# HGRN2 by running decay products and a state per 128 tokens, its levels spread between the other projections of the mixers

## The chip, the cores and the metric

One core of a Trainium2 chip runs the whole program. The metric is the device time of one execution in microseconds (us); lower is better. The engines are PE (TensorE, matrix products; PEld is its weight load), DVE (VectorE), ACT (ScalarE), POOL (GpSimd) and SP (SyncE, which here only issues DMAs). Each works through its own queue in order and waits for the others on semaphores.

## What is computed

A decoder of two layers over 512 tokens of width 1024, in fp32. Each layer is a gated MLP half step, four token mixers that share one input projection, a second half step, and a per-layer embedding:

```python
for l in range(DEPTH):
    h = h + 0.5 * swiglu(rmsnorm(h, ffn1_norm[l]), ...)
    z = rmsnorm(h, mix_norm[l]) @ w_in[l]
    (c_q, c_kv, k_pe, z_u, z_v, hq, hf, hi, hg, rq, rk, rv, rg) = jnp.split(z, ...)
    y_a = mla_mixer(c_q, c_kv, k_pe, ...)
    y_b = spatial_gating_mixer(z_u, z_v, ...)
    y_c = hgrn2_mixer(hq, hf, hi, hg, lb_all[l], hg_norm[l])
    y_d = retention_mixer(rq, rk, rv, rg, ...)
    h = h + jnp.concatenate([y_a, y_b, y_c, y_d], axis=-1) @ w_out[l]
    h = h + 0.5 * swiglu(rmsnorm(h, ffn2_norm[l]), ...)
    h = h + (p[l] @ ple_w_proj[l]) * jax.nn.sigmoid(rmsnorm(h, ple_norm[l]) @ ple_w_gate[l])
```

HGRN2, the mixer that the change rewrites, has 4 heads with keys of 128 and values of 64. It is a gated linear recurrence whose decay differs for each key channel and token:

```python
forget = lb + (1.0 - lb) * sigmoid(f);  log_f = log(forget);  k = 1.0 - forget
b = cumsum(log_f)                                   # over the tokens
scores[t, s] = sum_k q[t, k] * exp(b[t, k] - b[s, k]) * k[s, k]      # s <= t
o = scores @ v;   o = o * rsqrt(mean(o * o) + EPS) * norm_g;   y = o * silu(g)
```

(The reference cuts this into chunks of 64 tokens with a state between them; the sum is the same.)

## The kernel before

Activations lie feature-major: a tile is 128 features by 512 tokens, the hidden state is 8 such tiles `h`. Every projection is fp32 in three passes of the fp32r type: weights and inputs are each split into a high and a low part, and `mm3` issues high x high, high x low, low x high (the lines 142 to 144). A 128-column chunk of a projection is 8 x 3 = 24 matmuls of 512 columns into one PSUM bank. Weights come in tiles of 128 x 1024 by SP's queue (two raw buffers), are rounded to `wh` by ACT (L132) and get their rest `wl` from DVE (L133), three buffers each. The PSUM pool "d" (4 banks) takes the dense products (tiles z, n, uq, uk, uv, y), the pool "m" (4 banks) all small ones. What is said of dense work below means those `mm3` matmuls.

A scheduler sets the order of each engine's queue by the order of the program text and by priority; what stands under `urgent()` goes ahead, and `after(i, j)` fixes i behind j on its engine.

`mixers(l, ...)` runs once a layer. Chunks of the transposed input projection (`winT`, tile z) are 0 to 7 for HGRN2's f and q, 8 to 11 for MLA's latents, 12 to 15 for retention's q and k, 16 to 19 for the gates; `natural(j)` makes 512 token-major columns (tile n, 96 matmuls), j = 0 for the values of HGRN2 and retention, j = 1 for the spatial gating. In program order: `hgrn_gates(0)` (heads 0 and 1: tiles q, k, and c, the log of the forget gate), the latents, the values, `hgrn_scores` and `values_out` of the first pair of heads, `ret_rot` (retention's rotated q and k, copied into head order by 16 DMAs of POOL), MLA's projections and attention, `hgrn_gates(1)`, retention, HGRN2's second pair of heads, the gates and group norm of retention, `natural(1)` and the spatial gating, the gates and group norm of HGRN2, and the output projection. The z chunks of `hgrn_gates(1)`, 96 matmuls, are what PE has to do between attention's steps, and the z chunks of later steps and `natural(1)` are what lies between the second pair's levels.

`hgrn_scores` works by nine levels of halving. At level lev, tokens stand in blocks of w = 2^lev, and the second of two neighbours takes scores against the first. The tile `lev` holds both sides: q times exp of the log decay since the block's start, k times exp of what is left to the block's end. A level needs two ACT Exps, two DVE products (L500, L504), one DVE subtraction (L502) and one POOL addition onto c (L508), then its small matmuls: up to level 4, 32 products of 32 x 32 (`near`, tile nr, merged into `sc` by a predicated copy, L510), then 16, 8, 4 and 4 larger ones (tile lv), copied by ACT into the score tile `hst`. `values_out` sums values over the scores: per pair of heads 8 products of the diagonal 128-token blocks (L349) and 6 of all later tokens (L355), columns 128 to 384.

Of the kernel before, what the change touches and what calls it, by code (L numbers as in the profile page):

```python
# [19 lines left out]
P = 128  # L20
# [21 lines left out]
LN_MIN = 2.0**-60  # L42

# gain columns of vecs
# [10 lines left out]
# columns of cst  # L55
# [6 lines left out]
def trunk(ctx, tc, xT, pT, pos, wgu, wdn, winT, winN, wout, wpg, wpp, wmla,  # L62
# [24 lines left out]
    def stile(name="st"):  # L87
        return tp.tile([P, 10, P], F32, tag="st", bufs=5, name=nm(name))
# [75 lines left out]
    def split(src, g=None, name="x"):  # L164
        """parts of src * g"""
# [9 lines left out]
    def rsqrt(src, n):  # L175
        """(src + EPS) ** -0.5 of a few columns: a first guess from the exponent, then Newton steps"""
# [15 lines left out]
    def row_rsqrt(acc, n, last=None, v=None):  # L192
        """rsqrt(mean + eps) on all partitions, from the summed squares"""
# [9 lines left out]
    def ln_rsqrt(q, n, r, last=None, vt=None):  # L203
        """(q / n + EPS) ** -0.5 of full rows, by Ln and Exp and a Newton step"""
# [10 lines left out]
    def columns(r, tag):  # L215
        """rows on all partitions to columns, token by token"""
# [7 lines left out]
    class Norm:  # L224
        """operands and scale of RMSNorm(h) @ W, filled chunk by chunk"""
# [72 lines left out]
    tabs = {}  # L298

    def tables():  # L300
# [5 lines left out]
        def sine(dst, inv, phase, turn):  # L306
            """sin(pos * inv + phase), the argument reduced to [-pi, pi]"""
# [33 lines left out]
    def values_out(st, diag, v, hh):  # L341
        """[2 heads x 64, tok]: sum over s of v[s] st[s, t], two heads side by side in the array"""
# [16 lines left out]
    def group_norm(os, vx, gates, gcol):  # L359
        """parts of RMS norm per head * gain * gate, both chunks of a mixer; os lacks the queries' scale vx ** -0.5"""  # L360
# [13 lines left out]
        res = []  # L374
        dve.tensor_tensor(y, y, gates, op=ALU.mult)
        for c in range(2):
            dve.scalar_tensor_tensor(y[:, c], y[:, c], vec[:, gcol + c:gcol + c + 1], rr[:, c], op0=ALU.mult, op1=ALU.mult)
            res.append(split(y[:, c], name="yT"))
        return res

    def mixers(l, norm, done):
# [4 lines left out]
        def tchunk(j, wait=None):  # L386
            w = weights(winT[l, j])
            o = dense("z")
            for k in range(KD):
                i = mm3(o, wpart(w, k * P), xpart(x[k]), k == 0, k == KD - 1)  # L390
                if wait is not None and k == 0:
                    after(i, wait)
            return o

        def scaled(dst, j, wait=None):
            o = tchunk(j, wait)
# [3 lines left out]
        def natural(j, evac, wait=None):  # L400
            os = [dense("n") for _ in range(NB)]
            for b in range(4):
                w = weights(winN[l, 4 * j + b])
                for i in range(NB):
                    for e in range(2):
                        k = 2 * b + e
                        m = mm3(os[i], xpart(x[k], i * P, P), wpart(w, e * T, T), k == 0, k == KD - 1)
                        if wait is not None and k == 0:
                            after(m, wait)
# [8 lines left out]
        # lower bounds of the forget gates  # L418
        lbv = vec[:, C_LB:]
        if l:  # L420
# [14 lines left out]
            omlb = sp.tile([P, 4], F32, tag="omlb", bufs=1, name="omlb")  # L435
            dve.tensor_scalar(omlb, lb, -1.0, 1.0, op0=ALU.mult, op1=ALU.add)

        def hgrn_gates(b, wait=None):
            """q, k and log forget of two heads"""
            q, kk, c = unit(name="q"), unit(name="k"), unit(name="c")  # L440
            for e in range(2):
                hh = 2 * b + e
                f, n0 = kk[:, e], c[:, e]
                scaled(f, 4 * b + e, wait)
                act.activation(n0, f, AF.Relu, scale=-1.0)
                i = act.activation(f, f, AF.Relu)
                ea, eb, ls = t2(name="ea"), t2(name="eb"), t2(name="ls")
# [4 lines left out]
                after(act.activation(ea, n0, AF.Exp, scale=-1.0), i)  # L452
                after(act.activation(eb, f, AF.Exp, scale=-1.0), i)
                dve.tensor_tensor(ls, ea, eb, op=ALU.add)
                act.activation(ls, ls, AF.Ln)
                if l:
                    dve.scalar_tensor_tensor(n0, eb, lb[:, hh:hh + 1], ea, op0=ALU.mult, op1=ALU.add)
                    dve.tensor_scalar(n0, n0, LN_MIN, None, op0=ALU.max)
                    act.activation(n0, n0, AF.Ln)
                    dve.tensor_tensor(n0, n0, ls, op=ALU.subtract)  # L460
                else:
                    dve.scalar_tensor_tensor(n0, n0, -1.0, ls, op0=ALU.mult, op1=ALU.subtract)
                dve.tensor_tensor(f, f, ls, op=ALU.add)
                act.activation(f, f, AF.Exp, scale=-1.0)
                if l:
                    act.activation(f, f, AF.Copy, scale=omlb[:, hh:hh + 1])
# [3 lines left out]
            return q, kk, c  # L470

        def hgrn_scores(q, kk, c):
            """scores of two heads by levels of halving: every decay is taken from a point between s and t"""
            st = [stile("hst") for _ in range(2)]
            for e in range(2):
                pool.memset(st[e][:, 0:4], 0.0)
            sc = tp.tile([P, 8, 32], F32, tag="sc", bufs=1, name=nm("sc"))

            def near(a, b_):
                o = mps("nr")  # L480
                for e in range(2):
                    for j in range(NB):
                        for g in range(4):
                            s_ = slice(j * P + 32 * g, j * P + 32 * g + 32)
                            n = (e * NB + j) * 32
                            pe.matmul(o[32 * g:32 * g + 32, n:n + 32], lhsT=a[:, e, s_], rhs=b_[:, e, s_],
                                      start=True, stop=True)
                return o[:, 0:256].rearrange("p (n t) -> p n t", n=8)

            dve.tensor_tensor(sc, near(kk, q), cs[:, K_D32:K_D32 + 32].unsqueeze(1).to_broadcast([P, 8, 32]), op=ALU.mult)  # L490
            for lev in range(9):
                w = 1 << lev
                tt = unit(name="lev")

                def view(z, side):
                    return z.rearrange("p e (n s w) -> p (e n) s w", s=2, w=w)[:, :, side, :]

                tot = view(c, 0)[:, :, w - 1:w].to_broadcast([P, T // w, w])
                act.activation(view(tt, 1), view(c, 1), AF.Exp)  # L499
                dve.tensor_tensor(view(tt, 1), view(tt, 1), view(q, 1), op=ALU.mult)  # L500
                if lev:
                    dve.tensor_tensor(view(tt, 0), tot, view(c, 0), op=ALU.subtract)  # L502
                    act.activation(view(tt, 0), view(tt, 0), AF.Exp)
                    dve.tensor_tensor(view(tt, 0), view(tt, 0), view(kk, 0), op=ALU.mult)  # L504
                else:
                    act.copy(view(tt, 0), view(kk, 0))
                if lev < 8:
                    pool.tensor_tensor(view(c, 1), view(c, 1), tot, op=ALU.add)  # L508
# [546 lines left out]
```

## Time and profile before

| | us |
|---|---|
| median of 3 runs | 2160.43 |
| lowest, highest | 2159.74, 2160.61 |
| span of the profiled execution | 2159.3 |
| PE busy in it | 2122.8 (98%) |
| DVE busy | 1196.8 (55%) |
| ACT busy | 836.0 (39%) |
| POOL busy | 63.3 (3%) |

The span is what the trace of one execution covers, from the first instruction to the end of the last. Busy times are sums over the whole span; stages with different limits are averaged in them. The mixers of the two layers lie at about 367 to 664 us and 1434 to 1733 us; all else in the span is half steps and embeddings, which are dense products from end to end.

A row of a timeline gives start, duration, engine, line, operation, the output tile and its inputs, and in brackets how long the engine had been idle and which instruction ended that. Matmuls overlap, so the time that one costs in a row of equals is the distance of two starts. An fp32 matmul of a small product leaves two records, so that 32 of them show as x64. [...]

### The profile page before, as it was taken

The numbers are of one execution on the slowest core, as the hardware profiler recorded it, in microseconds if no ns is written. First come the engines' busy times: TensorE is split into PE (matmuls) and PEld (weight loads), VectorE is DVE, ScalarE is ACT, GpSimd is POOL, SyncE is SP. The second block draws the span as 40 slices with busy tenths as digits, with TensorE's granted clock in tenths as the row PEclk, the third lists the DMA queues.
The fourth block names the chain that finished last, engine by engine and source line by source line (L and its number), as shares of the span: only waits on it lengthen the run. The fifth ranks groups of instructions, "written<-read, shape, count | busy, mean of one in ns | idle before, by whom it ended". The sixth has DMA issues, their size and how long they took to land.

```text
span 2159.3 us, 27281 instructions
## 1 busy us (share of the span) xinstructions
PE 2122.8 (98%) x11232; PEld 1723.4 (80%) x11232; DVE 1196.8 (55%) x1666; ACT 836.0 (39%) x1210; POOL 63.3 (3%) x81
## 2 busy tenths in 40 slices
PE   9999999999999999999999999999999999999997
PEld 7888888776678888888888888887766788888887
DVE  6743447576675444446744444476766744444476
ACT  6322224456654222224432222254465532222253
POOL 0000000030200000000000000000210000000000
PEclk9999999999999999999999999999999999999999
DMA  5333333322133333333333333332211333333332
GB/s 160 115 98 93 103 94 99 91 61 80 31 91 95 98 97 94 102 96 110 94 93 97 98 92 104 92 101 82 83 47 53 88 95 98 98 92 104 93 106 75
DMA packets 60925, 199.26 MB, mean 92 GB/s; under 512 B 7424, under 2 KB 11008, under 8 KB 60800
## 3 DMA queue, kind: packets, MB, share of 16 engines
q1 hardware_dynamic: 57104, 192.59, 30.3%
q10 hardware_dynamic: 2672, 2.82, 0.4%
q0 software_dynamic: 1024, 2.10, 0.4%
q8 instruction: 88, 1.44, 0.3%
q14 instruction: 37, 0.30, 0.0%
HBM read 193.29 MB, written 2.10 MB: 90 GB/s over the span
## 4 chain that ended last, share of the span: by engine, by line
PE 91%; DVE 5%; ACT 2%; issue 1%; DMA 0%; POOL 0%; POOLq 0%; SPq 0%; DVEq 0%; ACTq 0%
PE gu L143 15%; PE gu L144 15%; PE gu L142 15%; PE dn L143 7%; PE dn L142 7%; PE dn L144 7%; PE z L143 3%; PE z L144 3%; PE z L142 3%; PE pg L143 1%; PE pg L144 1%; PE pg L142 1%; PE n L142 1%; PE n L144 1%; PE n L143 1%
## 5 line engine op out<-in xcount | busy, mean ns | idle before, releaser
L132 ACT CAST wh<-wr 128x1024 fp32r<-128x1024 f32 (+1 forms) x359 | 370.3, 1031 | 1045.7 <-PE gu L143 393.3
L143 PE MATMUL gu<-x,wh 128*128 128x512 f32 x1408 | 548.3, 389 | 0.2 <-DVE x L172 0.2
L144 PE MATMUL gu<-x,wl 128*128 128x512 f32 x1408 | 547.9, 389 | 0.0
L142 PE MATMUL gu<-x,wh 128*128 128x512 f32 x1408 | 547.3, 389 | 0.5 <-ACT x L171 0.5
L133 DVE TENSOR_TENSOR wl<-wr,wh 128x1024 fp32r<-128x1024 f32 (+1 forms) x359 | 432.2, 1204 | 87.3 <-ACT wh L132 72.5
L143 PEld LDWEIGHTS gu<-x,wh 128*128 128x128 f32 x1408 | 264.3, 188 | 56.6 <-DVE x L172 1.7
L142 PEld LDWEIGHTS gu<-x,wh 128*128 128x128 f32 x1408 | 264.2, 188 | 56.3 <-ACT x L171 1.0
L144 PEld LDWEIGHTS gu<-x,wl 128*128 128x128 f32 x1408 | 264.3, 188 | 54.8
L142 PE MATMUL dn<-hid,wh 128*128 128x512 f32 x704 | 273.9, 389 | 0.0
L143 PE MATMUL dn<-hid,wh 128*128 128x512 f32 x704 | 273.9, 389 | 0.0
L144 PE MATMUL dn<-hid,wl 128*128 128x512 f32 x704 | 273.9, 389 | 0.0
L281 DVE TENSOR_TENSOR g<-g,gu 128x512 f32<-128x512 f32 x88 | 60.4, 688 | 278.5 <-PE gu L144 272.3
L279 DVE TENSOR_TENSOR g<-gu,r 128x512 f32<-128x512 f32 x88 | 60.7, 691 | 212.8 <-PE gu L144 212.7
L291 DVE TENSOR_TENSOR dn<-dn,rh 128x512 f32<-128x512 f32 x96 | 66.4, 692 | 185.8 <-PE dn L144 183.8
L142 PEld LDWEIGHTS dn<-hid,wh 128*128 128x128 f32 x704 | 132.1, 188 | 27.5
L144 PEld LDWEIGHTS dn<-hid,wl 128*128 128x128 f32 x704 | 132.1, 188 | 27.4
L143 PEld LDWEIGHTS dn<-hid,wh 128*128 128x128 f32 x704 | 132.1, 188 | 27.4
L143 PE MATMUL z<-x,wh 128*128 128x512 f32 x320 | 131.3, 410 | 0.0
L142 PE MATMUL z<-x,wh 128*128 128x512 f32 x320 | 131.3, 410 | 0.0
L144 PE MATMUL z<-x,wl 128*128 128x512 f32 x320 | 129.2, 404 | 0.0
L508 POOL TENSOR_TENSOR c<-c 128x512 f32<-128x512 f32 x32 | 42.1, 1317 | 1459.7 <-ACT lev L499 1425.1
L142 PEld LDWEIGHTS z<-x,wh 128*128 128x128 f32 x320 | 61.6, 192 | 14.4 <-issue 2.3
(327 smaller groups left out, 2397.7 us busy)
## 6 DMA issues: line engine op xcount, KB each, us to landing
wr<-in_wgu SPq DMA_DIRECT2D x172, 512.0 KB, 3.6
wr<-in_wdn SPq DMA_DIRECT2D x64, 448.0 KB, 3.3
wr<-in_winT SPq DMA_DIRECT2D x40, 512.0 KB, 3.6
wr<-in_wdn SPq DMA_DIRECT2D x32, 512.0 KB, 3.5
wr<-in_winN SPq DMA_DIRECT2D x16, 512.0 KB, 3.6
wr<-in_wout SPq DMA_DIRECT2D x16, 512.0 KB, 3.6
wr<-in_wpg SPq DMA_DIRECT2D x16, 512.0 KB, 3.6
h<-in_xT SPq DMA_DIRECT2D x8, 256.0 KB, 4.9
```

The costliest lines, as they stand in the source:

```text
L132: act.copy(hi[:, :cols], raw[:, :cols])
L133: dve.tensor_tensor(lo[:, :cols], raw[:, :cols], hi[:, :cols].bitcast(F32), op=ALU.subtract)
L142: i = pe.matmul(o, lhsT=a[0], rhs=b[0], start=start, stop=False)
L143: pe.matmul(o, lhsT=a[0], rhs=b[1], start=False, stop=False)
L144: pe.matmul(o, lhsT=a[1], rhs=b[0], start=False, stop=stop)
L279: dve.tensor_tensor(g, ps[0], r, op=ALU.mult)
L281: dve.tensor_tensor(g, g, ps[1], op=ALU.mult)
L291: dve.tensor_tensor(t, o, rh, op=ALU.mult)
L508: pool.tensor_tensor(view(c, 1), view(c, 1), tot, op=ALU.add)
```

## The change

HGRN2 no longer takes logs of the decays. `hgrn_gates` makes k and the forget gate f itself, and all four heads' gates come at the start of the mixers. A class `Hgrn` holds a pair of heads: its q and k tiles are multiplied in place, level by level, by products of decays (q by the decay of the block before, k by that of the block behind), and the products d of neighbouring blocks give the next level's. Each level then is the small matmuls and, behind them, two DVE products and a tiny one for d; ACT's Exps and POOL's additions go. There are seven levels, within 128 tokens. Beyond, `out` transposes k (tile kt), makes for the first three blocks of 128 tokens a 128 x 64 state k v (tile kv), runs a recurrence over the blocks on DVE (tile hs), and adds to 8 products of the diagonal blocks 6 of a state with q.

```diff
+            def level(self, lev, wait):          # small matmuls of q, k; then, in place:
...
+                dve.tensor_tensor(view(q, 1), view(q, 1), d[:, :, 0:1].to_broadcast([P, n, w]), op=ALU.mult)
+                dve.tensor_tensor(view(k, 0), view(k, 0), d[:, :, 1:2].to_broadcast([P, n, w]), op=ALU.mult)
+                nxt = self.d2[:, self.at:self.at + n]
+                dve.tensor_tensor(nxt.unsqueeze(2), d[:, :, 0:1], d[:, :, 1:2], op=ALU.mult)
...
+            def out(self, v):
...
+                    for j in range(NB - 1):
+                        pe.transpose(o[:, j * P:(j + 1) * P], k[:, e, j * P:(j + 1) * P], ident)
+                    act.copy(kt[:, e, 0:384], o[:, 0:384])
...
+                        pe.matmul(kv[:, e, j], lhsT=kt[:, e, j * P:(j + 1) * P],
+                                  rhs=v(j)[:, (2 * b + e) * HV:(2 * b + e + 1) * HV], start=True, stop=True)
...
+                        dve.scalar_tensor_tensor(s[:, e, j], s[:, e, j - 1], self.d[:, e * NB + j:e * NB + j + 1],
+                                                 kv[:, e, j], op0=ALU.mult, op1=ALU.add)
...
+                        end = pe.matmul(o[e * HV:(e + 1) * HV, c], lhsT=v(j)[:, hh * HV:(hh + 1) * HV],
+                                        rhs=self.st[:, e, c], start=j == 0, stop=False)
...
+                        end = pe.matmul(o[e * HV:(e + 1) * HV, c], lhsT=s[:, e, j - 1], rhs=q[:, e, c],
+                                        start=False, stop=j == NB - 1)
```

The dense work of the latents, the values and retention's rotation becomes a generator that yields after every 12 matmuls, 24 steps in all; levels of the two pairs are placed between its steps in turn, one every 1.4 steps, and the two `out`s follow. `natural(1)` is moved up to stand as PE's work between attention's steps, with a plain evacuation; its Gelu is applied in place once attention's last Exp is through, and before retention's ACT work. The Silu of the gates comes behind the Gelus, and `group_norm` leaves the product with the gates to `gated` at the end. The pool of score tiles goes from 5 buffers to 4, that of `sc` from 1 to 2.

```diff
+        hg = [hgrn_gates(b) for b in range(2)]
...
+        for n, i in enumerate(dense_steps()):
+            if n < 2:
+                continue
+            if n == 2:
+                hgs = [Hgrn(b, *hg[b], i) for b in range(2)]
+            while todo and (14 - len(todo)) * 1.4 + 2 <= n:
+                lev, b = todo.pop(0)
+                hgs[b].level(lev, i)
...
+        for _ in natural(1, ev_uv):
+            pass
+        for i in range(NB):
+            gelu_end = act.activation(UV(i), UV(i), AF.Gelu)
+            after(gelu_end, exp_end)
...
-            act.activation(UV(i), o, AF.Gelu, scale=rc[0][:, i:i + 1])
-        natural(1, ev_uv, hg_end)
...
+                after(act.activation(G[m][:, e], G[m][:, e], AF.Silu), gelu_end)
+
+        yTd, yTc = gated(yd, G[1]), gated(yc, G[0])
```

On PE, at levels 1 and 2 of the first pair of heads in layer 0, before. The names: nr is a level's PSUM tile, lev its decayed q and k, z a chunk of retention's rotation.

```order
L486 MATMUL nr480_3203<-lev479_3196 32x32 x32
L143 MATMUL z500_3463<-x368_2533,wh498_3459 128x512
...
L144 MATMUL z500_3463<-x382_2607,wl499_3460 128x512
L486 MATMUL nr482_3244<-lev481_3237 32x32 x32
L142 MATMUL z504_3494<-x333_2349,wh502_3490 128x512
```

After, the same engine at three blocks in a row (lines of the changed kernel; n is a token block of the values, q and k the tiles multiplied in place; q418 and k419 are the second pair of heads, q393 and k394 the first).

```order
L503 MATMUL nr498_3431<-q418_2799,k419_2800 32x32 x32
L142 MATMUL n492_3362<-wl501_3471,x347_2422 128x512
...
L143 MATMUL n493_3363<-wh500_3470,x354_2459 128x512
L503 MATMUL nr502_3498<-q393_2639,k394_2640 32x32 x32
L141 MATMUL n490_3360<-wh504_3537,x361_2496 128x512
...
L143 MATMUL n491_3361<-wh504_3537,x368_2533 128x512
L503 MATMUL nr506_3553<-q418_2799,k419_2800 32x32 x32
```

Before, 8 dense matmuls stand between two blocks of one pair of heads here; after, 11 and 12 stand between blocks of different pairs, and so 23 between two of one pair.

PE at the end of HGRN2 in the changed kernel, where MLA's projection (tile uq) begins: kt are the transposes, kv the states' products, hst the scores, hs the states, ov the output; the suffixes tell the first pair of heads from the second.

```order
L564 MATMUL kt546_3980<-cs_85,k394_2640 128x128 x3
L141 MATMUL uq570_4096<-x450_2993,wh563_4084 128x512
...
L143 MATMUL uq571_4104<-x450_2993,wh563_4084 128x512
L569 MATMUL kv547_3985<-v443_2959,kt544_3974 128x64 x2
...
L587 MATMUL ov549_3998<-q393_2639,hs548_3992 64x128 x4
...
L564 MATMUL kt552_4027<-cs_85,k419_2800 128x128 x3
L141 MATMUL uq571_4104<-x464_3143,wh563_4084 128x512
L569 MATMUL kv553_4032<-v443_2959,kt550_4021 128x64 x2
...
L587 MATMUL ov555_4045<-q418_2799,hs554_4039 64x128 x4
```

Both pairs' outputs now stand here, one behind the other, and the dense products between them are the first 7 of MLA's query projection; before, one pair's output stood here and the other's after retention.

ACT behind attention in layer 0, before: rst are retention's scores, k and ls tiles of the second pair's gates.

```order
L132 CAST wh701_4625<-wr700_4623 128x1024
L455 ACTIVATE ls619_3979<-ls619_3979 128x512
L446 ACTIVATE k611_3941<-k611_3941 128x512
L452 ACTIVATE ea628_4054<-c612_3942 128x512
L453 ACTIVATE eb629_4055<-k611_3941 128x512
L586 COPY rst635_4096<-ro637_4103 128x384
L590 COPY rst635_4096<-ro638_4106 128x384
```

After: uv are the tiles of the spatial gating, n the PSUM tiles of `natural(1)`.

```order
L793 ACTIVATE uv652_4406<-n656_4410,rc391_2635 128x512
L131 CAST wh723_4796<-wr722_4794 128x1024
L798 ACT_TABLE_LOAD
L798 ACTIVATE uv651_4405<-uv651_4405 128x512 x2
L798 ACTIVATE uv652_4406<-uv652_4406 128x512 x2
L623 COPY rst669_4539<-ro671_4546 128x384
L627 COPY rst669_4539<-ro672_4549 128x384
```

A table load and the four Gelus have moved ahead of the first copy of retention's scores, and the second pair's gates are gone from here.

## Rows read from the trace of the kernel before

**Rows 1.** Page, part 1: busy us, share of the span, instructions.

```profile
PE 2122.8 (98%) x11232; PEld 1723.4 (80%) x11232; DVE 1196.8 (55%) x1666; ACT 836.0 (39%) x1210; POOL 63.3 (3%) x81
```

**Rows 2.** Timeline of PE: start, us, what; dense matmuls in a row.

```profile
386.02 0.39 PE L144 MATMUL z<-x,wl 128*128 128x512 f32 x1
...
404.61 0.39 PE L142 MATMUL z<-x,wh 128*128 128x512 f32 x1
```

**Rows 3.** Windows, tile z: stretch, length, PE (count), PEld, DVE, ACT, clock, DMA.

```profile
437.11:479.65 42.54, 26.32 (x96) 19.18 (x96) 3.84 (x6) 0.00 (x0) 0.92 0.21 57
549.06:574.72 25.66, 10.25 (x33) 6.42 (x33) 0.68 (x1) 0.00 (x0) 0.93 0.08 24
1504.86:1546.69 41.83, 25.21 (x96) 18.53 (x96) 3.84 (x6) 0.00 (x0) 0.96 0.21 59
1619.03:1647.10 28.07, 8.34 (x29) 4.97 (x29) 1.36 (x2) 0.00 (x0) 1.00 0.13 40
```

**Rows 4.** Windows, tile n: stretch, length, PE (count), PEld, ACT, clock, DMA.

```profile
1619.03:1647.10 28.07, 3.12 (x10) 1.80 (x10) 0.00 (x0) 1.00 0.13 40
```

**Rows 5.** Timeline of PE at HGRN2's levels, first pair of heads, layer 0.

```profile
445.34 1.08 PE L486 MATMUL nr<-lev 128*32 128x32 f32 x64 [2.58 <-DVE lev L504]
...
453.00 0.75 PE L486 MATMUL nr<-lev 128*32 128x32 f32 x64 [0.30 <-DVE lev L504]
453.68 0.50 PE L143 MATMUL z<-x,wh 128*128 128x512 f32 x1
454.02 0.40 PE L144 MATMUL z<-x,wl 128*128 128x512 f32 x1
```

**Rows 6.** Windows, all instructions: PE, PEld, DVE, ACT, POOL, clock, DMA share, GB/s.

```profile
445.00:450.00 5.00, 4.66 (x134) 3.71 (x136) 4.86 (x8) 1.90 (x3) 2.07 (x2) 0.66 0.04 13
...
400.00:437.00 37.00, 36.49 (x159) 28.81 (x157) 22.05 (x30) 13.52 (x19) 0.00 (x0) 1.00 0.32 95
```

**Rows 7.** Chain that ended last, first pair: start, us, step.

```profile
462.38 1.08 PE lv L528 x16
...
471.84 0.89 PE lv L538 x8
472.73 1.73 PE lv L546 x8
```

**Rows 8.** Timeline of PE: output of one pair, first record and what follows.

```profile
474.39 0.44 PE L349 MATMUL ov<-hst,v 128*64 128x128 f32 x4
...
477.23 0.50 PE L144 MATMUL z<-x,wl 128*128 128x512 f32 x1
```

**Rows 9.** Groups of instructions by form: count, busy us, mean ns, idle before.

```profile
L510 DVE COPY_PREDICATED sc<-mk,nr 128x256 f32<-128x256 uint8 x20 | 8.7, 433 | 0.0
...
L586 ACT COPY rst<-ro 128x384 f32<-128x384 f32 x8 | 3.8, 469 | 0.0
...
L133 DVE TENSOR_TENSOR wl<-wr,wh 128x1024 fp32r<-128x1024 f32 x293 | 360.9, 1232 | 82.2 <-ACT wh L132 72.5
```

**Rows 10.** Tile lev: line, count, least/median/most ns, from when to when.

```profile
L500 DVE TENSOR_TENSOR lev<-lev,q x36: 676/680/1757, 437.3 to 1631.1; 128x512 f32<-128x512 f32 x36
```

**Rows 11.** Timeline of DVE: first operation after the latents' second mean.

```profile
412.83 0.69 DVE L619 TENSOR_SCALAR lt<-ms 128x512 f32<-128x512 f32 x1 [0.86 <-PE ms L618]
```

**Rows 12.** Timeline of PE: the latents' scale turned into columns.

```profile
422.19 0.66 PE L219 MATMUL rc<-cs,lr 128*128 128x128 f32 x4 [0.51 <-DVE lr L190]
```

**Rows 13.** Timeline of ACT: a weight cast, a table load, an activation.

```profile
614.17 1.06 ACT L132 CAST wh<-wr 128x1024 fp32r<-128x1024 f32 x1
615.25 1.28 ACT L743 ACT_TABLE_LOAD   x1
616.54 0.63 ACT L743 ACTIVATE g<-g 128x512 f32<-128x512 f32 x1
```

**Rows 14.** Timeline of PE: retention's first scores and its first output.

```profile
531.47 0.37 PE L582 MATMUL rd<-rh,rh 64*128 64x128 f32 x1
...
537.34 0.33 PE L349 MATMUL ov<-rst,v 128*64 128x128 f32 x2
```

More of the change, by code (lines that the diff above doesn't have):

```diff
@@ L384, in mixers, with tsteps @@
         rc = norm.rc
[L386 removed]
+        def tsteps(j):
             w = weights(winT[l, j])
@@ L390, in tchunk, with scaled, natural @@
                 i = mm3(o, wpart(w, k * P), xpart(x[k]), k == 0, k == KD - 1)
-                if wait is not None and k == 0:
-                    after(i, wait)
-            return o
-        def scaled(dst, j, wait=None):
-            o = tchunk(j, wait)
+                if k % 4 == 3:
+                    yield i
+            return o
+        def tchunk(j):
+            g = tsteps(j)
+            while True:
+                try:
+                    next(g)
+                except StopIteration as e:
+                    return e.value
+        def scaled(dst, j):
+            o = tchunk(j)
             with urgent():
                 dve.tensor_tensor(dst, o, r, op=ALU.mult)
-        def natural(j, evac, wait=None):
+        def natural(j, evac):
             os = [dense("n") for _ in range(NB)]
@@ L407, in natural @@
                         m = mm3(os[i], xpart(x[k], i * P, P), wpart(w, e * T, T), k == 0, k == KD - 1)
-                        if wait is not None and k == 0:
-                            after(m, wait)
+                    if i % 2:
+                        yield m
             with urgent():
@@ L469, in hgrn_gates, with __init__, near @@
                     act.copy(q[:, e], o)
[L470 to L479, printed above, removed]
+            return q, kk, ff
+        class Hgrn:
+            def __init__(self, b, q, kk, ff, wait):
+                self.b, self.q, self.k = b, q, kk
+                self.st = stile("hst")[:, 0:8].rearrange("p (e j) t -> p e (j t)", e=2)
+                pool.memset(self.st, 0.0)
+                self.sc = tp.tile([P, 8, 32], F32, tag="sc", bufs=2, name=nm("sc"))
+                dve.tensor_tensor(self.sc, self.near(wait),
+                                  cs[:, K_D32:K_D32 + 32].unsqueeze(1).to_broadcast([P, 8, 32]), op=ALU.mult)
+                dve.tensor_tensor(q, q, ff, op=ALU.mult)
+                self.d = ff.rearrange("p e t -> p (e t)")
+                self.d2 = stile("hd").rearrange("p a t -> p (a t)")
+                self.at = 0
+            def near(self, wait):
                 o = mps("nr")
@@ new lines, in latents @@
+        def latents():
+            cqx = []
+            acc = tp.tile([P, T], F32, tag="acc", bufs=1, name=nm("acc"))
+            for e in range(2):
+                o = yield from tsteps(10 + e)
+                with urgent():
+                    cqx.append(split(o, vec[:, g0 + e:g0 + e + 1]))
+                    if e == 0:
+                        act.activation(acc, o, AF.Square)
+                    else:
+                        sq = t2(name="sq")
+                        act.activation(sq, o, AF.Square)
+                        dve.tensor_tensor(acc, acc, sq, op=ALU.add)
+            o = yield from tsteps(8)
+            with urgent():
+                ckx = split(o, vec[:, g0 + 2:g0 + 3])
+                sq = t2(name="sq")
+                act.activation(sq, o, AF.Square)
+                v, t, rr = unit(name="lv"), unit(name="lt"), unit(name="lr")
+                for e, (a, n) in enumerate(((acc, 256), (sq, P))):
+                    q = mps("ms")
+                    pe.matmul(q, lhsT=onesr.bitcast(F32), rhs=a, start=True, stop=True)
+                    dve.tensor_scalar(t[:, e], q, 1.0 / n, None, op0=ALU.mult)
+                    dve.scalar_tensor_tensor(v[:, e], norm.vx, EPS, t[:, e], op0=ALU.mult, op1=ALU.add)
+                act.activation(t, v, AF.Ln)
+                act.activation(rr, t, AF.Exp, scale=-0.5)
+                newton_step(v, rr, t)
+                rkv = rr[:, 1]
+                tabq = t[:, 0]
+                dve.scalar_tensor_tensor(tabq, rr[:, 0], MLA_SCALE, tabs["m"], op0=ALU.mult, op1=ALU.mult)
+                rkvc = columns(rkv, "rkvc")
+            op_ = yield from tsteps(9)
+            with urgent():
+                tr = t2(name="tr")
+                dve.tensor_tensor(tr[64:P], tabs["m"][64:P], r[64:P], op=ALU.mult)
+                ta, tb = t2(name="ka"), t2(name="kb")
+                dve.tensor_tensor(ta[64:96], op_[64:96], tr[64:96], op=ALU.mult)
+                dve.tensor_tensor(tb[64:96], op_[96:128], tr[96:128], op=ALU.mult)
+                krot = t2(name="krot")
+                dve.tensor_tensor(krot[64:96], ta[64:96], tb[64:96], op=ALU.add)
+                dve.tensor_tensor(krot[96:128], ta[64:96], tb[64:96], op=ALU.add)
+            lat.update(cq=cqx, ck=ckx, rkv=rkv, tabq=tabq, rkvc=rkvc, krot=krot)
@@ L788, in mixers @@
             yTb.append(split(o, name="yT"))
-        yTc = group_norm(oc, norm.vx, gates(0, hg_end), C_HG + 2 * l)
+        G = {}
+        for m in (1, 0):
+            G[m] = unit(name="g")
+            for e in range(2):
+                scaled(G[m][:, e], 16 + 2 * m + e)
+                after(act.activation(G[m][:, e], G[m][:, e], AF.Silu), gelu_end)
+        yTd, yTc = gated(yd, G[1]), gated(yc, G[0])
         yT = yTa + yTb + yTc + yTd
```

239 lines of the change are left out of this document (100 added, 139 removed).

## Prediction

> **What bounds the kernel now.** I read the page first: PE is busy 2122.8 of 2159.3 us, 98% [rows 1]. Nothing can be won by making another engine faster; time goes only where PE stands still or runs something other than its dense products. So I looked for PE's dense pace, then for the stretches that fall short of it. The pace: from 386.02 to 404.61 us 82 dense matmuls of 512 columns follow each other, (404.61 - 386.02) / 82 = 0.2267 us each [rows 2]. Next, the windows in which HGRN2's levels run, two per layer: 42.54, 25.66, 41.83 and 28.07 us, 138.10 in all [rows 3]. In them stand 96 + 33 + 96 + 29 matmuls of tile z [rows 3] and 10 of tile n [rows 4], 264 at 0.2267 = 59.85 us. So **78.25 us** go to the small products of the levels and to waits around them. The page's busy share hides this, since PE counts as busy within a chain of small products.
>
> What the waits look like: at 445.34 a level's block of products comes after 2.58 us of idle, released by the level's last DVE product; later blocks wait 0.30 and the like [rows 5]. [...]
>
> **The change, part by part.** *Products of the levels.* With the clock full, a block of the finest levels takes from 453.00 to 453.68 = 0.68 us [rows 5] (each small fp32 matmul leaves two records, so 32 show as 64). After the change 28 such blocks remain, 7 for each pair of heads and layer (level 5 has fewer matmuls of the same kind and is priced as one): 28 x 0.68 = 19.0. Level 6 takes 1.08 per pair [rows 7]: 4.3. The two top levels, 0.89 and 1.73 per pair [rows 7], go. In their place come per pair 6 transposes, 6 state products of 64 columns, and 14 output products of 128 columns. Output before: 28 records from 474.39 to 477.23, 2.84 us [rows 8], 0.10 each. Transposes: 24 x 0.10 = 2.4. State products, 48 records at two thirds of that, 0.0675: 3.2. Output: 3584 columns against 5120 in the two passes, 4 x 2.84 x 0.7 = 8.0 (at most 11.4, if each costs what one costs now). Each small block also breaks the dense row once: the first dense matmul behind one takes 454.02 - 453.68 = 0.34 instead of 0.23 [rows 5], 32 x 0.11 = 3.6. Sum 19.0 + 4.3 + 2.4 + 3.2 + 8.0 + 3.6 = **40.5 us**, against 78.25: 37.7 us less if no wait comes.
>
> *Waits at the levels.* Each level now stands about 12 dense matmuls (2.7 us) behind the last, and the two pairs take turns, so a pair has some 5.4 us for what follows a block: a predicated copy (0.43 [rows 9]) and two products over half of 128x1024, 0.68 each [rows 10] = 1.8. POOL's adds, beside which the same products have taken up to 1.76 [rows 10], are gone. Does DVE keep up as a whole? In 400 to 437 us, latents and values without levels, it was busy for 22.05 [rows 6]. To this come per layer 14 x 1.36 + 10 x 0.43 = 23.3 for the levels, five more weight splits at 1.23 [rows 9] = 6.2, twelve products of the rotation at 0.68 = 8.2, and 10 for the initial products, the small products of the decays and the values' means, an estimate by the same 0.68 and 0.43 for some 17 operations: 70. PE needs for the same stretch 24 steps of 12 at 0.2267 = 65.3, plus 11.7 of small blocks and 1.8 of breaks, 79. DVE fits, at some 90%, with little to spare. Where it bunches is the latents' chain: from 412.83 to the columns' transposes at 422.19 it takes 9.4 [rows 11, 12], and PE waited 0.51 there. Now level work is queued into that chain on DVE (0.43 + two times 0.68 = 1.8 more, 11.2), while PE has 44 dense matmuls, 10.0, ahead of its transposes: 1.2 instead of 0.5. With as little again where the first blocks come, I put **2.0** for both layers.
>
> *The end of HGRN2 and the start of attention.* The chain transposes, ACT copy (0.47 [rows 9]), state products, DVE recurrence, output runs twice, with only 7 dense matmuls of tile uq between. Behind it in DVE's queue stand the group norm's scaling and then the evacuations of q and k, on which attention's first scores wait. The rotated copies' DMAs, issued by POOL, are moved up, too; through reused buffers some of those evacuations wait for them. The trace of before has no such place. Between 0 (all under dense work) and 8 us (two chains of two copies and four small DVE operations, twice) I take **3.5**, nearer to the 2.58 of the worst wait seen per layer than to the sum.
>
> *natural(1).* As cover for attention its 96 dense matmuls take the place of the 96 of the second pair's gates; equal, so nothing. But on ACT, behind attention's last product, now stand a cast, four evacuations, a weight cast, a table load and four Gelus ahead of the first copy of retention's scores: the last evacuation waits for the last of 11 dense matmuls, 2.5 + 0.63, then 1.06 + 1.28 + 4 x 0.63 [rows 13] + 0.47 = 8.5. On PE in the same time: 2.5 for the 11, five of six products of a pair of heads (531.47 to 537.34, less 5 dense between, 4.7 [rows 14], five sixths 3.9), one dense 0.2: 6.6. Then the sixth needs the PSUM bank that this copy frees. 1.9 per layer: **3.8** (bounds 0 and 6). The Gelus hide nothing else, and if these scores needed no bank, the wait would move on to the output products behind 6 dense matmuls and vanish.
>
> [...]
>
> *The tail.* Gates' Silu and the gating products come together at the end, after the spatial gating's chain, where before the gates' chunks lay under the levels; their 96 matmuls are cover for that chain still. **1.0** (bounds 0 and 3). The extra Exp and two DVE products per head in the gates lie under 24 dense matmuls per chunk, 5.4 us: nothing. Fewer stile buffers (4 instead of 5) only matter in attention, where two pairs hold four: nothing.
>
> Sum: 2.0 + 3.5 + 3.8 + 1.0 = 10.3 of new waits, 37.7 - 10.3 = **27.4 us gained**. The profiled execution has 2159.3; the median of the runs is 1.1 above it. 2159.3 - 27.4 + 1.1 = **2133**.
>
> **The rivals.** *Half late.* DVE is at 90%, and between the levels' products stand weight splits of 1.23 and products of the rotation, in an order fixed by priority and not by time. If every second of the 28 blocks waits half of what the worst waited, 14 x 1.29 = 18 more: 2151. Against it: the waits of now come where a level makes ACT, DVE and POOL each pass over its data before its products, and where a pair has some 8 to 16 dense matmuls between its blocks, not 24.
> *No new wait.* ACT and DVE catch up everywhere: 2160.4 - 37.7 = 2123. Against it: the two short covers named above.
> *Slower: the levels are bound by DVE.* In-place products make every block wait for the product before it, and weight splits queued behind late ones hold the dense work as well. If each of the 28 blocks waits the full 2.58 [rows 5], 72 us: 2160.4 - 37.7 + 72 = 2195. It decides from 37.7 / 28 = 1.35 us per block on. For it speaks the 4.86 of 5.00 in [rows 6]; against it that a block has its dense cover between.
> *Not done as said:* the levels are not spread. The order of the program shows 12 dense matmuls between blocks, so this is excluded but for what a late weight DMA does; SP's queue moves the same bytes.
>
> **How the numbers follow.** Forecast 0.62 (2133), half late 0.15 (2151), no new wait 0.10 (2123), slower 0.08 (2195), and 0.05 for a mixture that ends within 0.2% of now, which is about what a measurement of this kernel can tell from no change. Bounds: no waits, 2120 with 2.5 for the prices of small products; all upper bounds, 2 + 8 + 6 + 3 = 19, gain 18.7, 2142, and half late on its upper side 2152. Range 2120 to 2152, which leaves out the last two. Faster 0.87, same 0.05, slower 0.08.
>
> **What would show it.** Windows of the levels: one stretch per layer of about 79 us with 288 dense matmuls, and clock full in it. Waits before blocks (tile nr) under 0.5 us; if they are 1 us or more at half of the blocks, half late holds, if at all and above 1.35, the slower. The transposes rc: idle near 1. Behind attention: ACT's Gelus ahead of the copies to rst, and PE idle before the third score product, near 1.9; zero or over 4 would make that term wrong. Tile kv, hs and the first sc: idle of some 1.7 per layer in all. POOL's adds gone, and no product of a level above 0.8. A fall of the granted clock in attention or retention would make the sum wrong, since each term is at full clock.

## The result

The changed kernel takes **2128.19 us** (2127.80 to 2129.94) against 2160.35 of the kernel before: ratio 0.9852, 95% interval 0.9838 to 0.9866. The prediction said 2133 with a range of 2120 to 2152. The profiled executions span 2127.8 and 2159.3 us, 31.5 apart. The page's first part after, to be laid beside [rows 1]:

```profile
PE 2108.7 (99%) x11240; PEld 1717.2 (81%) x11240; DVE 1174.4 (55%) x1686; ACT 781.6 (37%) x1123; POOL 21.1 (1%) x45
```

Of the 31.5, 14.1 are PE's busy time (2122.8 less 2108.7); the rest is idle time that PE no longer has. What PE waited for from the start of the first mixers to the end of the second ones (engine, line, releaser: us in total, times, longest; "issue" is a wait for which the profile shows no releaser), before, the largest rows and two that are needed below:

```profile
PE nr L486 <- DVE lev L504: 8.8, 5, 2.6
PE nr L486 <- DVE sc L490: 4.7, 2, 2.4
PE lv L517 <- issue: 1.6, 1, 1.6
PE lv L517 <- ACT gt L364: 1.1, 1, 1.1
PE rc L219 <- DVE lr L190: 1.0, 2, 0.5
PE nr L486 <- DVE sc L510: 1.0, 1, 1.0
PE ro L588 <- DVE rst L583: 1.0, 1, 1.0
...
PE sg L777 <- DVE vn L771: 0.7, 2, 0.4
PE y L142 <- ACT yT L168: 0.5, 2, 0.3
...
```

and after, all rows:

```profile
PE uv L141 <- ACT va L749: 1.8, 2, 0.9
PE nr L503 <- issue: 1.7, 1, 1.7
PE nr L503 <- DVE k L548: 0.8, 2, 0.4
PE rc L218 <- DVE lr L189: 0.7, 2, 0.3
PE uq L141 <- DVE qh L734: 0.4, 2, 0.2
PE oa L785 <- ACT pt L778: 0.2, 1, 0.2
```

The waits before blocks for DVE, 8.8 + 4.7 + 1.0, are down to 0.8. The levels' stretch after, by windows (length, PE, PEld, DVE, ACT, POOL with counts, granted clock, DMA share, GB/s; compare [rows 3, 6]):

```profile
420.00:499.00 79.00, 76.51 (x1126) 59.51 (x1125) 56.37 (x90) 26.23 (x53) 4.05 (x8) 0.98 0.28 78
1471.00:1550.00 79.00, 78.24 (x1141) 61.14 (x1140) 59.64 (x98) 27.85 (x55) 3.92 (x8) 1.00 0.28 84
```

Where the four stretches of [rows 3] had a clock of 0.92, 0.93, 0.96 and 1.00, these have 0.98 and 1.00 of full; what lowers it is time at half (in the first of the four it is 0.50 from 445.50 to 448.50 us and from 459.00 to 462.30). DVE is busy for 56.4 and 59.6 of 79 us, not for the 70 that the prediction added up; one reason is that it added durations, and in a row products of 0.68 start 0.60 apart (at 444.01 and 444.61 on DVE before).

### The profile page after: what moved, and what is told of

Same layout as the page of the kernel before. It is cut to its first block, busy times and chain, and to the rows that moved or that the text cites. A ratio compares the mean times of both kernels' runs of the same rounds, so it can differ in the third digit from the quotient of the medians.

```text
span 2127.8 us, 27180 instructions
## 1 busy us (share of the span) xinstructions
PE 2108.7 (99%) x11240; PEld 1717.2 (81%) x11240; DVE 1174.4 (55%) x1686; ACT 781.6 (37%) x1123; POOL 21.1 (1%) x45
## 4 chain that ended last, share of the span: by engine, by line
PE 96%; DVE 2%; ACT 1%; issue 1%; DMA 0%; DVEq 0%; ACTq 0%; SPq 0%
PE gu L142 15%; PE gu L143 15%; PE gu L141 15%; PE dn L143 8%; PE dn L141 7%; PE dn L142 7%; PE z L141 4%; PE z L142 3%; PE z L143 3%; PE pg L143 1%; PE pg L142 1%; PE pg L141 1%; PE y L141 1%; PE y L142 1%; PE y L143 1%; PE n L142 1%
## 5 line engine op out<-in xcount | busy, mean ns | idle before, releaser
L143 PEld LDWEIGHTS dn<-hid,wl 128*128 128x128 f32 x704 | 132.2, 188 | 27.4
L141 PEld LDWEIGHTS dn<-hid,wh 128*128 128x128 f32 x704 | 132.2, 188 | 27.4
L141 PE MATMUL z<-x,wh 128*128 128x512 f32 x320 | 128.4, 401 | 0.0
L142 PE MATMUL z<-x,wh 128*128 128x512 f32 x320 | 127.2, 398 | 0.0
L143 PEld LDWEIGHTS z<-x,wl 128*128 128x128 f32 x320 | 60.5, 189 | 13.4 <-issue 1.0
```

## The experiments

### What made the levels late before

**e1** leaves out all of a level but its products and copies (the scores lack all decay).

```diff
-                act.activation(view(tt, 1), view(c, 1), AF.Exp)      # and every other pass over tt and c
...
-                    dve.copy_predicated(sc, mk[:, lev]..., near(tt, tt))
+                    dve.copy_predicated(sc, mk[:, lev]..., near(kk, q))
```

> The kernel before, with everything per level left out but the small matmuls and the copies of their results: no Exps, no products with decays, no subtraction, no POOL addition (the scores then lack all decay). Same matmuls, same order of the program text. Theory (the gain is mostly waits taken away): of the 78.3 us beyond dense work in the four stretches, 28 x 0.69 + 4 x (1.07 + 0.89 + 1.73 + 2.84) + breaks 4 = 49 are products, so 29 are waits and half clock; without them 2160.4 - 29 = 2131. Rival (the gain is mostly fewer and smaller products): waits are under 15, and this stays at 2145 or above.

Measured: 2149.83, ratio 0.9951 (0.9936 to 0.9966). The time lies where the rival had it (2145 or above), but for a reason that neither theory had. Hardly any other engine is waited for any more, so the products stand in one row of six blocks, and there PE stops with no releaser; its timeline, and a window behind it:

```profile
436.60 2.22 PE L486 MATMUL nr<-q,k 128*32 128x32 f32 x231
440.83 1.33 PE L486 MATMUL nr<-q,k 128*32 128x32 f32 x128 [2.00 <-issue]
445.38 0.55 PE L486 MATMUL nr<-q,k 128*32 128x32 f32 x25 [3.22 <-issue]
...
446.00:452.00 6.00, 6.00 (x60) 5.60 (x55) 0.44 (x1) 4.37 (x16) 0.00 (x0) 0.59 0.02 4
```

No releaser is named: the waits are "issue", 11.9 us in six of them over both layers, and behind them the mean granted clock of 6 us is 0.59 of full. e1 is no floor for the products and doesn't decide between the two theories; it says that blocks side by side have a price of their own. What PE stops for is read in the last section.

**e4** takes POOL's additions of log decays out of the kernel before (the scores lack their decay) and touches nothing else.

```diff
-                if lev < 8:
-                    pool.tensor_tensor(view(c, 1), view(c, 1), tot, op=ALU.add)
...
-                    act.activation(view(tt, 0), view(tt, 0), AF.Exp)
+                    act.activation(view(tt, 0), view(tt, 0), AF.Exp, scale=0.0)
```

> The kernel before without POOL's additions of log decays (the scores then lack their decay; one Exp gets the scale 0 so that numbers stay in range, at the same cost). If POOL's additions make DVE's products late (up to 1.76 us for 0.68), DVE's 36 longest come down and the waits at blocks fall by about half: 2150 to 2155. If the passes of ACT and DVE alone make the blocks late, 2158 to 2161.

Measured: 2138.62, ratio 0.9899 (0.9884 to 0.9914): 22 us, more than twice what was expected at best and about two thirds of the change's gain, with ACT's and DVE's other passes and the levels' place in the program as they were (the scheduler may set single instructions otherwise). Part 1 of its page, to be laid beside [rows 1]:

```profile
PE 2117.4 (99%) x11232; PEld 1720.1 (80%) x11232; DVE 1175.6 (55%) x1666; ACT 838.3 (39%) x1213; POOL 21.5 (1%) x49
```

DVE makes the same 1666 operations in 1175.6 us, not 1196.8: 21.2 us of what had counted as DVE's busy time were not work.

**e5** is e4 with an addition per level kept on POOL, but into a scratch tile from which no level reads.

```diff
-                    pool.tensor_tensor(view(c, 1), view(c, 1), tot, op=ALU.add)
+                    px_ = t2(name="px")
+                    pool.tensor_tensor(px_.rearrange("p (n w) -> p n w", w=w), view(tt, 1), tot, op=ALU.add)
```

> As e4, but POOL still makes an addition of 512 columns per level, into a scratch tile that nothing waits for but later scratch tiles (the scores lack their decay, as in e4). If the additions hurt because DVE stands still while POOL runs (in the kernel before one such product took 1.76 us for 0.68), most of e4's gain of 22 is lost: 2152 to 2160. If they hurt because the next level's Exp waits for the sum of decays, the gain stays: 2137 to 2142.

Measured: 2161.38, ratio 1.0008 (0.9999 to 1.0017). All of e4's gain is lost, and DVE's busy time is back at 1197.5 us, though nobody needs what POOL adds: it is not the chain through c. One dependence is left: at four Exps ACT waits for POOL, which reads the tile lev, 9.0 us in all, so that e5 alone would leave up to 9 of the 22 to such waits. The tile views of e4 and then e5 (line, count, least/median/most ns; compare [rows 10]):

```profile
L500 DVE TENSOR_TENSOR lev<-lev,q x36: 676/684/696, 437.1 to 1610.1; 128x512 f32<-128x512 f32 x36
```

```profile
L500 DVE TENSOR_TENSOR lev<-lev,q x36: 673/679/1984, 436.8 to 1632.8; 128x512 f32<-128x512 f32 x36
...
L509 POOL TENSOR_TENSOR px<-lev,c x32: 1056/1552/3660, 437.6 to 1631.5; 128x512 f32<-128x512 f32 x32
```

With POOL's additions a product of this line takes up to 1984 ns, without them never above 696. The timeline of the kernel before shows how; POOL's addition, then DVE:

```profile
441.94 1.46 POOL L508 TENSOR_TENSOR c<-c 128x512 f32<-128x512 f32 x1 [0.75 <-ACT lev L499]
```

```profile
440.34 1.93 DVE L133 TENSOR_TENSOR wl<-wr,wh 128x1024 fp32r<-128x1024 f32 x1
442.20 1.23 DVE L650 TENSOR_SCALAR s<-s 128x4 f32<-128x4 f32 x1
```

A scaling of 4 columns takes 1.23 us and ends at 443.43, when POOL's addition ends (441.94 + 1.46 = 443.40). In e6, where no addition runs on POOL, the same operation:

```profile
440.66 0.16 DVE L650 TENSOR_SCALAR s<-s 128x4 f32<-128x4 f32 x1
```

This DVE operation is held while POOL runs, and the profile books that as DVE's busy time. Not every one is: POOL's next addition runs from 446.64 to 448.11, and in its midst a predicated copy, which reads a level's products from PSUM, takes its usual 0.43:

```profile
447.02 0.43 DVE L510 COPY_PREDICATED sc<-mk,nr 128x256 f32<-128x256 uint8 x1
```

So what the traces show is a hold of some operations: 1.23 against 0.16 for the scaling, up to 1.76 against 0.68 for products of two SBUF tiles [rows 10], and nothing for this copy from PSUM. What decides which are held, no run here shows.

**e6** is the kernel before with one word changed, and the same results.

```diff
-                    pool.tensor_tensor(view(c, 1), view(c, 1), tot, op=ALU.add)
+                    dve.tensor_tensor(view(c, 1), view(c, 1), tot, op=ALU.add)
```

> The kernel before with its additions of log decays on DVE in place of POOL, one word of the source; same results. DVE gets 8 x 0.68 more per pair of heads, but no POOL operation runs beside it. If what POOL took from DVE is the cause of the waits, 2138 to 2145. If DVE's load per level is the cause (the theory of the prediction), DVE at 4.9 of 5.0 us gets more and the waits grow: 2165 to 2175.

Measured: 2142.44, ratio 0.9918 (0.9902 to 0.9935), 17 us less than before. Part 1 of its page:

```profile
PE 2118.7 (99%) x11232; PEld 1718.4 (80%) x11232; DVE 1196.6 (56%) x1698; ACT 830.3 (39%) x1205; POOL 21.4 (1%) x49
```

DVE makes 32 operations more, some 20 us of work, in the same busy time as before. ACT's Exps wait for the sums of decays as long as they did (22.0 us for DVE's, 21.4 for POOL's before), and the kernel is faster all the same. So it was POOL's hold on DVE that made the levels late; the chain through c and DVE's load can account for the 4 us between e6 and e4 at most.

### What the new place and the cheap passes are worth

**e2** puts the old passes back into the changed kernel; **e9** does so without the POOL addition.

```diff
-                dve.tensor_tensor(view(q, 1), view(q, 1), d[:, :, 0:1].to_broadcast([P, n, w]), op=ALU.mult)
+                pool.tensor_tensor(p1_, view(q, 0), d[:, :, 0:1].to_broadcast([P, n, w]), op=ALU.add)   # e2 only
+                act.copy(p1_, d[:, :, 0:1].to_broadcast([P, n, w]))
+                dve.tensor_tensor(view(q, 1), view(q, 1), p1_, op=ALU.mult)
+                dve.tensor_tensor(p0_, view(k, 1), d[:, :, 1:2].to_broadcast([P, n, w]), op=ALU.subtract)
+                act.copy(p0_, d[:, :, 1:2].to_broadcast([P, n, w]))                 # then k by p0_
```

> The changed kernel, with the work that a level had before put back beside its own: two ACT passes, a third DVE product and a POOL addition per level, all over 512 columns, the two products waiting for ACT; same results. Theory (what counts is that 12 dense matmuls lie between blocks): the cover takes it, 2128 to 2132. Rival (what counts is fewer passes per level): DVE gets 14 x 0.68 = 9.5 more per layer and POOL's additions make its operations longer; the blocks come late, 2140 or more.

> As e2 (the changed kernel with two ACT passes and a third DVE product per level put back), but without the POOL addition; same results. If e2's 7 us were POOL's hold on DVE: 2128 to 2130, like the changed kernel. If they were the longer chain by ACT and the third product: 2133 to 2136, like e2.

Measured: e2 2135.40, ratio 0.9885 (0.9869 to 0.9902); e9 2129.63, 0.9858 (0.9844 to 0.9871). ACT's two passes and DVE's third cost some 1.4 in the new place, within the noise, POOL's addition 5.8. In those 5.8 stands more than the hold, since in e2 ACT's copy writes the tile that POOL wrote and so waits for it. In the old place the addition cost 17 to 22 (e6, e4). e2's extra waits are at blocks and in the latents' chain:

```profile
PE nr L503 <- DVE k L554: 3.4, 4, 1.3
PE rc L218 <- DVE lr L189: 2.5, 2, 1.3
```

**e3** takes the place away and leaves the cheap passes.

```diff
-            while todo and (14 - len(todo)) * 1.4 + 2 <= n:
+            while todo:
```

> The changed kernel with all 14 levels of a layer set behind the third dense step, so that only 2 to 4 dense matmuls stand between blocks; all else is the same. Theory (cover counts): each pair's block needs 1.8 us of DVE and gets some 0.6 to 1.1 of dense cover and the other pair's 0.7, so PE waits about 1 us at 10 of 14 blocks per layer, and the chain of the latents comes later: +12 to +20, 2140 to 2148, with the clock granted at half in places. Rival (cheap passes count, place doesn't): within 4 of the changed kernel, 2132 at most.

Measured: 2135.64, ratio 0.9885 (0.9870 to 0.9900): 7.4 more than the changed kernel, less than the cover theory wanted, more than its rival did, and for neither's reason. Hardly a block waits for DVE:

```profile
PE nr L503 <- issue: 5.5, 7, 1.6
...
PE z L143 <- issue: 1.7, 1, 1.7
PE z L141 <- issue: 1.1, 1, 1.1
```

It is "issue" again, 8.3 us against 1.7 in the changed kernel, as in e1, where blocks of small products stand close together. What spreading gives is mostly this: it keeps them apart.

**e7** adds two copies to DVE's work at each level of the changed kernel.

```diff
-                dve.tensor_tensor(view(q, 1), view(q, 1), d[:, :, 0:1].to_broadcast([P, n, w]), op=ALU.mult)
+                    dve.tensor_tensor(s0, view(z, side), d[:, :, 1 - side:2 - side].to_broadcast([P, n, w]), op=ALU.mult)
+                    dve.tensor_copy(view(z, side), s0)        # for q and for k
```

> The changed kernel with each of the two products of a level made of two DVE operations (a product into scratch, then a copy back): 14 x 1.36 = 19 us more of DVE per layer, the chain behind a block 3.2 us instead of 1.8 of some 5.4. The stretch of the levels has DVE busy for 62 to 66 of 91 us. By these measured loads DVE still fits (85 of 91) and the time rises by 2 to 6, from the bunched places alone: 2130 to 2134. By the prediction's estimate (70 of 79 already) DVE would be over its limit by 10 per layer: 2145 or more.

Measured: 2129.02, ratio 0.9858 (0.9843 to 0.9873), not to be told from the changed kernel. A copy took 0.42 and not 0.68, so DVE is busy for 65.9 and 68.0 of the two stretches of 79, some 9 us more per layer, not 19. The rivals "half late" and "slower" needed DVE to be near its limit; it takes up these 9 us without a loss that can be measured.

### Terms of the sum, and a faster kernel

**e10** evacuates natural(1) through the Gelu at once, four ACT passes fewer ahead of retention.

```diff
-            act.activation(UV(i), o, AF.Copy, scale=rc[0][:, i:i + 1])
+            gelu_end = act.activation(UV(i), o, AF.Gelu, scale=rc[0][:, i:i + 1])
+            after(gelu_end, exp_end)                          # and no Gelu in place
```

> The changed kernel with the Gelu back in natural(1)'s evacuation (one ACT pass instead of two per tile, still behind attention's last Exp), so four passes of 0.63 fewer lie ahead of the first copy of retention's scores. By the prediction's term (PE waits 1.9 per layer there): -3 to -4, 2124.5. By the changed kernel's trace (only 0.2 to 0.3 of idle there): within 1, 2127 to 2129.

Measured: 2128.94, ratio 0.9856 (0.9842 to 0.9869). Nothing stood there to win.

**e8** sets the two pairs' blocks of a level side by side; **e11** also moves the second half of HGRN2's group norm behind attention; **e12** also moves the levels two steps later and takes e10's Gelu.

```diff
-            while todo and (14 - len(todo)) * 1.4 + 2 <= n:
+            while todo and (14 - len(todo)) // 2 * 3 + 2 <= n:      # e12: + 4
...
-        yc = group_norm(oc, norm.vx, C_HG + 2 * l)
+        yc1 = group_norm1(oc, norm.vx)                              # e11, e12: copy, square, mean
...
+        yc = group_norm2(*yc1, C_HG + 2 * l)                        # behind attention: Ln, Exp, Newton, scaling
```

> The changed kernel with the two pairs' blocks of one level side by side, every third dense step, so that the dense row is broken 7 times per layer for the levels instead of 14. A break costs 0.11 by the prediction, 0.25 by the sums over runs of 12 dense matmuls in the changed kernel's trace: 14 fewer give 1.5 to 3.5, 2124.7 to 2126.7. Rival: 64 small products twice in a row let PE's own supply of instructions run dry (a gap that the profile calls issue stood at 423 us behind the only place with such a row), +1.7 at each of some of the 14 places: 2130 to 2140.

> e8 with the second half of HGRN2's group norm (Ln, Exp, Newton step, scaling) put behind attention in the program text, so that ACT's evacuations of attention's values no longer stand behind it (PE waited 0.9 for them per layer in e8). If that wait was on the path: 2.0 less than e8, 2123. If attention's first step only waits for something else next: 2124.5 to 2125.5.

> e11 with the levels two dense steps later (so that the first three blocks don't stand in one row; PE's supply gap of 1.9 in layer 0 came there) and with e10's Gelu. If the gap comes from that row: 1.9 less than e11, 2121. If the gap comes from the code that PE meets there for the first time: as e11, 2122.5 to 2124. Later levels in the latents' chain could cost 0.5 to 1 per layer.

Measured: e8 2125.16, ratio 0.9838 (0.9823 to 0.9853); e11 **2121.43**, 0.9822 (0.9808 to 0.9835); e12 2121.72, 0.9822 (0.9809 to 0.9836). e8 came as expected: two blocks in a row stop PE hardly more than before ("issue" 1.9 against 1.7), and half of the breaks go, 3.0 us for 14 of them. e11 is 3.7 below e8, where 2.0 were expected; the rest is not traced. In e11 one kind of wait is left of the table above:

```profile
PE nr L509 <- issue: 2.6, 2, 1.6
```

e12's "issue" is shorter (1.0 and 0.2), but its later levels run into the latents' chain, and nothing is gained:

```profile
PE ms L664 <- DVE acc L655: 1.2, 2, 0.6
PE rc L218 <- DVE lr L189: 1.0, 2, 0.5
PE nr L509 <- issue: 1.0, 1, 1.0
PE nr L509 <- DVE k L554: 0.8, 2, 0.4
```

## Why the prediction was right, and where its steps were not

**The frame held.** The time beyond dense work in the four stretches [rows 3, 4] was 78.25, and replacing it by a sum of products and waits gave the right size: 27.4 forecast, 32.2 measured. But in it the products are some 4.5 too cheap, the named waits some 6.4 too dear, and stops of PE that cost some 3.3 are missing. That these three nearly cancel is luck.

**The products were too cheap.** A block takes what was said, 459.32 - 458.63 = 0.69. But it breaks the dense row on both sides; PE's timeline after, at two blocks 12 dense matmuls apart and at the first pair's states:

```profile
458.63 0.76 PE L503 MATMUL nr<-q,k 128*32 128x32 f32 x64
459.32 0.50 PE L141 MATMUL n<-wh,x 128*128 128x512 f32 x1
459.66 0.39 PE L142 MATMUL n<-wl,x 128*128 128x512 f32 x1
...
461.95 0.39 PE L143 MATMUL n<-wh,x 128*128 128x512 f32 x1
462.27 0.76 PE L503 MATMUL nr<-q,k 128*32 128x32 f32 x64
...
1552.89 1.45 PE L569 MATMUL kv<-v,kt 128*128 128x64 f32 x12
1554.26 1.09 PE L582 MATMUL ov<-hst,v 128*64 128x128 f32 x16
...
1555.72 0.33 PE L564 MATMUL kt<-cs,k 128*128 128x128 f32 x1
```

The dense matmul behind a block takes 0.34, the one ahead of the next 462.27 - 461.95 = 0.32, so a break is 0.20, not 0.11: 32 x 0.20 = 6.4 where 3.6 stood. The 0.20 agrees with e8, where 14 breaks fewer saved 3.0. The states' 12 records take 1554.26 - 1552.89 = 1.37, 0.114 each, not the 0.0675 scaled by columns: 5.5 for 48 where 3.2 stood. The output's first 24 records take 1.46, 0.061 each, a little less than scaled (0.071). Sum some 45, not 40.5.

**The waits were too dear.** The latents, 2.0 forecast: 0.7 at rc, less than the 1.0 of before, and 0.8 at two blocks. The start of attention, 3.5: 1.8 + 0.4. The place is the one named, behind the group norm, but the engine mostly another: the prediction had DVE's evacuations of q and k, which are the 0.4; the 1.8 are ACT's evacuations of the values (tile va), behind the group norm's Exps in ACT's queue. e11 moves these, and the waits are gone. Retention, 3.8: none. Here one step failed. ACT's chain was nearly right: attention's last product ends where dense work resumes at 560.35, and ACT's first copy ends 8.3 later (8.5 said). PE and ACT there:

```profile
566.90 0.70 PE L625 MATMUL ro<-rh,rh 64*128 64x256 f32 x2
567.44 0.38 PE L626 MATMUL ro<-rh,rh 64*128 64x128 f32 x2
```

```profile
568.23 0.46 ACT L623 COPY rst<-ro 128x384 f32<-128x384 f32 x1
```

PE makes the sixth product at 566.90, 6.55 after the end of attention (6.6 said), 1.3 before that copy begins. It does not wait for the bank that the copy frees, as the prediction had it; which bank it took, the trace doesn't say. e10 confirms that the chain isn't on the path. The tail, 1.0: none.

**A term was missing.** The sum had no stop of PE without a releaser, and each of its terms was at full clock. The changed kernel has one such stop, of 1.7 at 423 us, and behind it, from 425.30 to 428.80, the granted clock is 0.51: eight dense matmuls take 3.5 there (0.43 from start to start), some 1.6 more than at full clock.

**What the miss of 4.8 is.** With these measurements the sum is 45 of products, 3.9 of named waits and 3.3 for the stop: 52 in place of the forecast's 50.8, a gain of 26. So some 6 of the measured 32.2 lie outside the four stretches, where the prediction counted nothing. Before's waits in retention and behind it, which went as well, make 2.5 of them (1.0 at ro, 0.7 at sg and 0.5 at y in the table above, and 0.3 more at ro); the rest is not traced.

**The reason was half wrong.** The prediction read DVE's 4.86 of 5.00 us [rows 6] as load per level, and priced cover. It saw the product of 1.76 us beside POOL [rows 10] and gave it no term. By e4 and e6 that hold is worth 17 to 22 us: taking POOL out in the old place, with all else as it was, gives over half of the gain. Of the 4.86, too, some 0.6 were standing still (a product of 1.30 at 447.35, beside POOL's addition). The new place with the new products gives 25, even with POOL's additions in it (e2), since there the cover hides most of the hold: the two overlap, and their gains don't add. The sum came out right since it replaced the whole 78.25 and never needed to know why that was lost. A forecast for e6 from the same theory was wrong in sign.

**The rivals.** "Half late" and "slower" fell by the changed kernel's own trace, in which two blocks wait 0.4 each for DVE, and by e7. "No new wait" (2123) is as far from 2128 as the forecast, on the other side: it has no waits where 3.9 and the stop stand, and the same products, too cheap.

## What to carry to other kernels

A busy DVE next to a running POOL may be a held DVE (here 1.23 us for a scaling of 0.16): compare the longest and the median duration of one form of instruction before calling it load, and try the POOL operation on another engine before rewriting the algorithm. Where PE stops without a releaser, count its instructions from stop to stop. Spread small products in blocks of one or two through the dense work; in long rows of them PE ran out of instructions (stops of 11.9 us in e1), and each block broke the dense row on two sides (0.20 us), so set blocks that are ready together side by side. A sum that replaces a whole stretch can be right for the wrong reason; only an experiment that removes one suspect shows which it was.

## What the runs showed of the hardware

In rows of small fp32 products PE stops with no releaser: 11.9 us in e1, 8.3 in e3 (2.8 of it at dense matmuls), up to 3.5 at once (e1). A stop of 1.7 is left in the changed kernel where three blocks of 32 stand within 2.5 us of each other, but in layer 0 alone; layer 1 has the same blocks and none.

The traces show what PE stops for. The page of the changed kernel has this row among its DMA queues (packets, MB, share):

```profile
q8 instruction: 88, 1.44, 0.3%
```

These are 88 packets of 16 KiB, and PE's 11240 matmuls and 11240 weight loads make 255 for each, so this is taken for the queue that brings PE's instructions. All kernels' traces together have 29 stops of PE of over 0.3 us without a releaser. 28 of them stand where, counted from the start of the program, a next group of 256 matmuls and weight loads begins (at the same place of the group, or one record beside it). And each of the 28 ends 1.2 to 1.6 us after a packet of q8 has landed, the packet with the number of that group. So PE stops for its next instructions, which are not there yet. In e1, 128 small records with their 128 weight loads run in 1.33 us between two stops, from 440.83 on, while the two packets landed 4.4 us apart, at 439.61 and 444.00. The same number of dense matmuls takes 128 x 0.2267 = 29 us, and ahead of the mixers the packets land some 30 us early. In layer 1 of the changed kernel groups begin at 1475.64 and 1482.73, and their packets had landed 8.5 and 4.4 us before.

Where dense matmuls stand alone none of this is seen: from 655 to 1419 us, between the two layers' mixers, the profile of the changed kernel lists no wait of PE. In the rows of small ones of e1 one such stop lasted 3.5 us.
